# A trunk layer in split fp32: the order of down's steps, activations by two blocks, and two homes for the gates' x pairs

## The chip, the cores and the metric

The kernel runs on one core of one Trainium2 chip. The metric is device time in microseconds of one execution. The engines are named as the profile names them: PE (TensorE, matmuls; PEld its weight loads), DVE (VectorE), ACT (ScalarE), POOL (GpSimd) and SP (SyncE). On PE, DVE and ACT instructions run in program order; SP and POOL issue most of the DMA transfers, each from an in-order queue of its own, some are issued by ACT.

## What is computed

One layer of a transformer trunk for 512 tokens of width 2048, in float32:

```python
proj = rmsnorm(x, norm_mix) @ w_in        # q, k, v of two attentions, gates ga and gb (2048 columns each)
...
merged = sigmoid(ga) * (out_a @ w_branch_a) + sigmoid(gb) * (out_b @ w_branch_b)
x = x + merged @ w_out
u = rmsnorm(x, norm_ffn) @ w_up           # 2048 -> 2 x 5632
u = up[:, :-2] * cw[0] + up[:, 1:-1] * cw[1] + up[:, 2:] * cw[2] + conv_b
gate, val = split(u)
x = x + (silu(gate) * val) @ w_down       # 5632 -> 2048
```

Tokens lie along the free dimension (512), features along the 128 partitions.

## The kernel before

**Split operands.** Each float32 operand of a matmul is kept as two parts, hi (rounded to fp32r) and lo (the rest), and each product is three matmuls: hi by hi, hi by lo, lo by hi. Weights are split after loading by an ACT cast (`wh`) and a DVE subtraction (`wl`), L672 and L673, or L773 and L774 for plain tiles. Activations are split in the same way.

**Units.** From the gates on, the work of PE goes by units: 256 rows of a weight matrix by 512 columns, against a pair of feature tiles (256 features by 512 tokens). `tiles_by_halves` computes a unit plainly, in 2 x 4 x 2 blocks with three matmuls of 128x256 each, 48 in all. `products` does it by seven products of a Strassen-Winograd form, 7 x 2 x 3 = 42 matmuls of 128x256. For this the weights get three sums (`sums`, L630: two operations of 128x256 and one of 128x512 on DVE) and the activations come in seven forms, of which three are values and four sums (`forms`, L701 to L714). A run of units accumulates in one PSUM group per product; after its last unit `combine` (L810 to L850) makes the four quarters of the result out of the seven products, on ACT and DVE.

**Weights ahead of use.** `advance` moves the units through loading (`f`, SP queue, four buffers), sums and preparation (`prep`, two parities of w buffers, so that unit u + 2 is prepared when PE has finished unit u). A unit that is "kept" has its sums made early, in windows of the attention and branch stages: POOL fetches its weights (L645), DVE adds (L649), ACT stores the sums in DRAM (`sums...`). Later it loads 256 + 128 KB of weights and 512 KB of sums, in place of 512 KB of weights.

**Stages.** Attention and its projections (matmuls of 128x512), the gates' first three column blocks by plain 128x512 units, the other five blocks by `gate_products`, the branches and `w_out` by plain tiles, up (22 steps of 8 units, seven products), down (88 units).

- Gates: while the third block runs, `form_h` (L900) makes the seven forms of the eight x pairs: it scales a pair (ACT, L898), forms and splits it, and then lets POOL load the pair after the next into a buffer of the tag "a" (`load_x`, L890; two buffers). `gate_to_quad` (L884) multiplies PE's banks on DVE (L875), takes the sigmoid on ACT (L876) and stores.
- Up: each step writes eight blocks of activations (four values, four sums) of one pair to DRAM, `act0` to `act21`, by way of a convolution and a SiLU whose operations are queued behind the next step's units (L1054 to L1119).
- Down: the 22 pairs are in three parts (0 to 6, 7 to 13, 14 to 21), the output in four column blocks n. `load_act` brings a pair from DRAM into slots, one 128x256 block at a time (SP queue), and `split_act` (L1100 ACT, L1101 DVE) splits each block in place. Before, for each part the four blocks follow each other; three runs, (part 0, n 0), (part 0, n 3) and (part 1, n 3), are plain. The results of parts 0 and 1 are added to `total` in DRAM by accumulating POOL transfers (L1170); part 2 adds `total` on DVE and writes out.

**Order.** A scheduler with a timeline of its own orders the instructions; those under `keep` stay in the order in which the program issues them. The hooks `before(i)` and `after(i)` put loads and splits around unit i of a run.

Of the kernel before, what the change touches and what calls it, by code (L numbers as in the profile page):

```python
# [11 lines left out]
F32 = mybir.dt.float32  # L12
# [27 lines left out]
def trunk_kernel(  # L40
# [666 lines left out]
    def forms(src):  # L707
        y, one, two = form_sums(src)
        all_ = y[:, 0], y[:, 2], two[:, 1], one[:, 1], one[:, 0], two[:, 0], y[:, 3]
        res = [slot(F32R) for _ in all_]  # L710
        for i in (0, 1, 6, 4, 3, 5, 2):
            v, o = all_[i], res[i]
            nc.scalar.copy(o[:, :256], v)
            nc.vector.tensor_tensor(o[:, 256:], v, o[:, :256].bitcast(F32), ALU.subtract)  # L714
        return res

    def products(w, pairs, acts, evac, before=None, after=None, kept=(), total=None):

        n = len(pairs)

        def run():
            ps = []
            for i in range(n):
                if before:
                    before(i)
                u = next_unit()
                for f in (0, 1, 2, 3, 5, 6, 4) if i == n - 1 else range(7):
                    if i == 0:
                        ps.append(bank("mm"))
                    (wh, wl), a = u.parts[f], acts[i][f]  # L730
                    for m in range(2):
                        o, s = ps[f][:, m * 256:(m + 1) * 256], slice(m * P, (m + 1) * P)
                        mm(o, wh[:, s], a[:, :256], i == m == 0, False)
                        mm(o, wh[:, s], a[:, 256:], False, False)
                        last["pe"] = mm(o, wl[:, s], a[:, :256], False, i == n - 1 and m == 1)
# [45 lines left out]
    def tiles_by_halves(w, pairs, acts, evac, before=None, after=None):  # L781


        n = len(pairs)

        def run():
            ps = [bank("mm") for _ in range(4)]
            for i in range(n):
                if before:
                    before(i)  # L790
                u = next_unit()
                y = [acts[i][j] for j in (0, 7, 1, 6)]
                for m in range(4):
                    c = slice(m * P, (m + 1) * P)
                    for b in range(2):
                        first, last = i == b == 0, i == n - 1 and b == 1
                        wh, wl = u.hi[:, b, c], u.lo[:, b, c]
                        for t in range(2):
                            o, a = ps[m][:, t * 256:(t + 1) * 256], y[2 * b + t]
                            mm(o, wh, a[:, :256], first and t == 0, False)  # L800
                            mm(o, wh, a[:, 256:], False, False)
                            mm(o, wl, a[:, :256], False, last and t == 1)
                advance()
                run_queued(1)
                if after:
                    after(i)
            evac(ps)

        steps.append(run)
        for i in range(n):  # L810
            units.append(TilesByHalves(w[pairs[i]], len(units)))
            products_.append(units[-1])
# [75 lines left out]
            nc.gpsimd.dma_start(gate_a[m // 2], held["g"])  # L888

    def load_x(j):  # L890
        held[j] = quad("a")
        nc.gpsimd.dma_start(
            held[j], x_t[2 * j * P:(2 * j + 2) * P].rearrange("(a p) n -> p a n", p=P))

# [6 lines left out]
    def form_h():  # L901

        j = len(hf)
        if j < KD // 2:
            scale_x(j)
            hf.append(forms(held.pop(j)))
            if j + 2 < KD // 2:
                load_x(j + 2)

    def pre_forms():  # L910
        end_attention()
        load_x(0)
        load_x(1)

    def before_forms(kb):
        if 0 < kb < 7:
# [179 lines left out]
    def split_act(part, n):  # L1096
        if 0 <= n < len(parts[part]):
            for o in acts[part][n]:
                hi, lo = o[:, :256], o[:, 256:]
                keep(nc.scalar.copy(hi, lo.bitcast(F32)))  # L1100
                keep(nc.vector.tensor_tensor(  # L1101
                    lo, lo.bitcast(F32), hi.bitcast(F32), ALU.subtract))
# [42 lines left out]
    def down(part, n):  # L1145
        held = []

        def before(i):
            if n == 0 and part:
                load_act(part, 6 + i)  # L1150
            if part == n == 0 and i == 4:
                run_queued(1)
            if part == 0 and n == 1 and i == 1:
                queue.extend(unfinished)
            if part < 2 and n == 3:
                load_act(part + 1, i - 1)
            if part == 2 and i == 4:
                for j in range(2):
                    held.append(quad("ao"[j]))
                    dma(held[j], total[2 * n + j])  # L1160

        def after(i):
            if n == 0:
                split_act(part, i + (5 if part else 2))
            if part < 2 and n == 3:
                split_act(part + 1, i - 2)

        def evac(*results):
            for j, r in enumerate(results):
# [11 lines left out]
                keep(nc.scalar.copy(res[m // 2][:, m % 2], ps[m]))  # L1181
            evac(*res)

        if (part, n) in PLAIN:
            view = w_down.rearrange("(d b p) (s n) -> s d p b n", b=2, p=P, s=4)
            tiles_by_halves(view[n], parts[part], acts[part], evac_plain, before=before, after=after)
        else:
            view = w_down.rearrange("(d b p) (s h n) -> s d p b h n", b=2, p=P, s=4, h=2)
            products(view[n], parts[part], acts[part], evac if part < 2 else evac_total,
                     before=before, after=after, kept=(0, 1) if part and n == 0 else (),  # L1190
                     total=held if part == 2 else None)
# [73 lines left out]
```

## Time and profile before

| | |
|---|---|
| median of 3 runs | 2466.1 us (2464.73 to 2466.31) |
| the profiled execution | 2463.77 us, of which the span is 2462.0 |
| matmul, 128x256, seven products and plain | 277 ns each by its record (start to start is shorter, they overlap) |
| `f<-in_w_down`, 256 KB | 133 loads, median 4.0 us from issue to landing |
| `f<-sums`, 512 KB | 88 loads, median 5.8 us |
| `s<-act`, 128 KB | 168 loads, median 4.4 us |
| mean of all DMA | 214 GB/s |

Times in the profile are microseconds from the start of the span. A row of the groups gives line, engine, operation, out<-in, count, then busy time, mean ns of one, and the idle time of the engine just ahead of it with what ended it. A row of the timeline gives start, duration, engine, line, and in brackets how long the engine had been idle and which instruction released it. A row of the chain gives start and duration of a piece of the chain that ended last. The stages lie at 0 to 540 (attention), to 800 (gates), to 1203 (branches and `w_out`), to 2006 (up) and to the end (down).

### The profile page before, as it was taken

The page shows a single profiled execution, that of the slowest core. Times are in us where ns is not written, and L with a number is a line of the kernel's source. Part 1 is how long each engine was busy: PE and PEld are TensorE (multiplying, and loading weights), DVE is VectorE, ACT ScalarE, POOL GpSimd, SP SyncE. Part 2 cuts the span into 40 slices and gives each one's busy share as a digit, 9 for nine tenths or more (in the row PEclk, how much of TensorE's full clock was granted, in tenths as well). Part 3 has the DMA queues.
Part 4 walks back from the last instruction along what each step waited for, and adds up shares of the span by engine and source line. Part 5 has one row for each costly group of instructions (what it writes and reads, how often), then busy time and mean ns, then how long its engine had stood idle before and what let it go on. Part 6 is the DMA issues. An engine that isn't in the chain of part 4 may idle for free.

```text
span 2462.0 us, 45471 instructions
## 1 busy us (share of the span) xinstructions
PE 2436.6 (99%) x17430; PEld 2277.2 (92%) x17430; DVE 1860.1 (76%) x2939; ACT 1283.2 (52%) x1936; POOL 329.0 (13%) x406
## 2 busy tenths in 40 slices
PE   9999999999999999999999999999999999999998
PEld 7888888888899888888999999999999999999998
DVE  6788776635788656557878888888888878696897
ACT  5255554445545322334666566665665656463643
POOL 1414133000000111110011011110111101000000
PEclk9999999999999999999999999999999999999999
DMA  5767777435555677766588887887888897775853
GB/s 198 246 232 251 252 258 268 161 124 188 185 166 173 209 271 253 238 235 227 161 210 229 220 233 215 226 231 219 229 222 215 230 287 194 206 201 147 250 164 128
DMA packets 312362, 526.43 MB, mean 214 GB/s; under 512 B 27600, under 2 KB 179536, under 8 KB 312144
## 3 DMA queue, kind: packets, MB, share of 16 engines
q1 hardware_dynamic: 226320, 320.68, 41.3%
q0 software_dynamic: 48384, 128.91, 21.3%
q10 hardware_dynamic: 37440, 73.94, 7.9%
q8 instruction: 136, 2.23, 0.4%
q14 instruction: 82, 0.67, 0.1%
HBM read 378.80 MB, written 98.57 MB: 194 GB/s over the span
## 4 chain that ended last, share of the span: by engine, by line
PE 92%; DMA 3%; issue 3%; DVE 1%; ACT 1%; POOL 0%; SPq 0%; ACTq 0%; DVEq 0%; POOLq 0%
PE mm L76 88%; PE tr L76 2%; DMA f<-in_w_down 1%; PE tr L530 1%; DMA a<-in_x_t 1%; PE tr L369 0%; DMA s<-act 0%; DVE s L1101 0%; DMA sums<-s 0%; DMA f<-in_w_in 0%; ACT wh L672 0%; DMA s<-in_w_in 0%; DMA out_b<-o 0%; ACT hi L160 0%; PE tr L423 0%
## 5 line engine op out<-in xcount | busy, mean ns | idle before, releaser
L76 PE MATMUL mm<-s,wh 128*128 128x256 f32 (+1 forms) x9620 | 1719.6, 289 | 12.3 <-ACT wh L672 7.8
L76 PEld LDWEIGHTS mm<-s,wh 128*128 128x128 f32 x9620 | 1429.6, 188 | 55.8 <-ACT wh L672 9.2
L76 PE MATMUL mm<-s,wl 128*128 128x256 f32 (+1 forms) x4810 | 1227.1, 289 | 0.0
L76 PEld LDWEIGHTS mm<-s,wl 128*128 128x128 f32 x4810 | 841.4, 188 | 20.1
L672 ACT CAST wh<-f 128x1024 fp32r<-128x1024 f32 (+1 forms) x566 | 519.1, 943 | 484.7 <-PE mm L76 344.6
L673 DVE TENSOR_TENSOR wl<-f,wh 128x1024 fp32r<-128x1024 f32 (+1 forms) x566 | 610.6, 1088 | 188.7 <-ACT wh L672 185.9
L630 DVE TENSOR_TENSOR f<-f 128x256 f32<-128x256 f32 (+1 forms) x585 | 298.6, 510 | 4.7
L76 PE MATMUL mm<-hi,s 128*128 128x512 f32 x896 | 286.1, 394 | 5.6 <-ACT hi L160 5.6
L774 DVE TENSOR_TENSOR wl<-f,wh 128x1024 fp32r<-128x1024 f32 x85 | 104.1, 1225 | 172.5 <-ACT wh L773 167.4
L773 ACT CAST wh<-f 128x1024 fp32r<-128x1024 f32 x85 | 89.2, 1050 | 246.9 <-PE mm L76 213.9
L161 DVE TENSOR_TENSOR lo<-raw,hi 128x1024 fp32r<-128x1024 f32 (+1 forms) x97 | 117.7, 1214 | 122.8 <-ACT hi L160 116.9
L76 PEld LDWEIGHTS mm<-hi,s 128*128 128x128 f32 x896 | 168.1, 189 | 38.7 <-ACT hi L160 5.6
L76 PE MATMUL mm<-s,hi 128*128 128x512 f32 x640 | 195.8, 392 | 0.0
L160 ACT CAST hi<-raw 128x1024 fp32r<-128x1024 f32 (+1 forms) x97 | 101.2, 1043 | 157.6 <-PE mm L76 146.6
L76 PE MATMUL mm<-lo,s 128*128 128x512 f32 x448 | 175.6, 393 | 0.0
L76 PEld LDWEIGHTS mm<-s,hi 128*128 128x128 f32 x640 | 119.4, 188 | 24.1 <-ACT hi L160 0.3
L1070 POOL DMA_DIRECT2D o<-a x44 | 52.9, 1202 | 600.4 <-ACT a L1069 482.9
L76 PE MATMUL mm<-s,lo 128*128 128x512 f32 x320 | 120.8, 392 | 0.0
L649 DVE TENSOR_TENSOR s<-s 128x256 f32<-128x256 f32 x236 | 98.0, 421 | 5.8 <-DMA s<-in_w_in 3.4
L76 PEld LDWEIGHTS mm<-lo,s 128*128 128x128 f32 x448 | 84.6, 189 | 16.0
L1067 ACT ACTIVATE o<-u,smalls 128x512 f32<-128x512 f32 x88 | 71.5, 812 | 23.2 <-ACT wh L672 12.5
L645 POOL DMA_DIRECT2D s<-in_w_up x86 | 62.2, 725 | 95.0 <-DMA sums<-s 56.7
(148 smaller groups left out, 1860.0 us busy)
## 6 DMA issues: line engine op xcount, KB each, us to landing
f<-in_w_up SPq DMA_DIRECT2D x281, 256.0 KB, 3.8
f<-sums SPq DMA_DIRECT2D x88, 512.0 KB, 5.8
o<-a POOLq DMA_DIRECT2D x88, 511.0 KB, 7.1
f<-in_w_down SPq DMA_DIRECT2D x133, 256.0 KB, 4.0
raw<-in_w_in SPq DMA_DIRECT2D x63, 512.0 KB, 3.6
sums<-s ACTq DMA_DIRECT2D x118, 256.0 KB, 2.7
s<-in_w_up POOLq DMA_DIRECT2D x86, 256.0 KB, 5.3
s<-act SPq DMA_DIRECT2D x168, 128.0 KB, 4.4
```

What stands on the lines that cost most here:

```text
L76: return nc.tensor.matmul(o, l, r, start=start, stop=stop, skip_group_check=True).ins
L160: nc.scalar.copy(hi[:, c:c + n], self.raw[:, c:c + n])
L161: nc.vector.tensor_tensor(lo[:, c:c + n], self.raw[:, c:c + n], hi[:, c:c + n].bitcast(F32), ALU.subtract)
L630: add = lambda *args: keep(nc.vector.tensor_tensor(*args, ALU.add))
L645: keep(nc.gpsimd.dma_start(x, self.w[:, b]))
L649: add = lambda *args: keep(nc.vector.tensor_tensor(*args, ALU.add))
L672: keep(nc.scalar.copy(hi, f))
L673: keep(nc.vector.tensor_tensor(lo, f, hi.bitcast(F32), ALU.subtract))
L773: keep(nc.scalar.copy(hi, self.f))
L774: keep(nc.vector.tensor_tensor(lo, self.f, hi.bitcast(F32), ALU.subtract))
L1067: keep(nc.scalar.activation(self.o[:, m], u[:, m], AF.Identity, bias=cb[:, i:i + 1], scale=cw[:, i, 1:2]))
L1070: keep(nc.gpsimd.dma_start(self.o[:, :, 1:], first[:, :, :S - 1], accum_op=ALU.add))
```

## The change

It has five parts.

1. Down runs in ten steps, each with a column block n and one part or two: (0; 0), (1; 0), (2; 0), (3; 0, 1), (2; 1), (1; 1), (0; 1, 2), (1; 2), (2; 2), (3; 2). Where two parts stand, their 14 or 15 units accumulate in one PSUM group. Only (0; 0) is plain.
2. Activations of down are loaded by two blocks (128x512, 256 KB), three such and a single block for parts 1 and 2. A second slot takes the hi part of a wide block. For part 0 the values are loaded in up's last step and in the first run, the sums in the first and second. For the part that comes next, `LOADS` and `SPLITS` name the units of the merged run at which a pair is loaded and split.
3. Up's steps 1 to 20 keep units 2 and 3, not 2, 3 and 7. In down the kept units are 0, 1, 2 of (1; 0) and 5, 6, 7, 9, 10, 11, 12 of each merged run.
4. The x pairs of the gates are loaded into buffers of the tags "a" and "u" in turn, four ahead.
5. Slices of the split activations are handed on as (hi, lo) pairs; the work is the same.

```diff
-PLAIN = ((0, 0), (0, 3), (1, 3))
+LOADS = 1, 2, 3, 5, 6, 7, 8, 9
+SPLITS = 3, 4, 5, 7, 8, 9, 10, 11
+AHEAD_OF_SPLITS = 5, 6, 7, 9, 10, 11, 12
...
     def load_x(j):
-        held[j] = quad("a")
+        held[j] = quad("au"[j % 2])
...
-            if j + 2 < KD // 2:
-                load_x(j + 2)
+            if j + 4 < KD // 2:
+                load_x(j + 4)
...
-        load_x(0)
-        load_x(1)
+        for j in range(4):
+            load_x(j)
...
-    def load_act(part, n):
+    FORM_OF = 0, 7, 1, 6, 4, 3, 5, 2
+    VALUES, SUMS = (0, 2), (4, 6)
+
+    def load_act(part, n, blocks=None):
...
-            blocks = (0, 2, 7, 5, 4, 6, 3, 1)[:8 - (part == 2)]
-            tiles = [slot(F32R) for _ in blocks]
-            for o, i in zip(tiles, blocks):
-                dma(o[:, 256:].bitcast(F32), act[parts[part][n]][:, i])
-            acts[part].append(tiles)
+            if n == len(acts[part]):
+                acts[part].append(([None] * 8, deque()))
+            for b in blocks or (2, 4, 6, 0):
+                o = slot(F32R)
+                c = slice(0, 512) if b or not part else slice(256, 512)
+                dma(o[:, c].bitcast(F32), act[parts[part][n]][:, b:b + (c.stop - c.start) // 256])
+                acts[part][n][1].append((b, o, c))
...
-                load_act(0, i - 1)
+                load_act(0, i - 1, VALUES)
...
-                split_act(0, i - 6)
+                split_act(0, i - 6, 2)
...
-                 before=before, after=after, kept=(2, 3, 7) if s else range(8))
+                 before=before, after=after,
+                 kept={0: range(8), pairs_ff - 1: (2, 3, 7)}.get(s, (2, 3)))
...
         def before(i):
-            if n == 0 and part:
-                load_act(part, 6 + i)
+            if n == part == 0:
+                load_act(0, i, SUMS)
+            elif len(run) > 1 and i in LOADS:
+                load_act(run[1], LOADS.index(i))
...
         def after(i):
-            if n == 0:
-                split_act(part, i + (5 if part else 2))
-            if part < 2 and n == 3:
-                split_act(part + 1, i - 2)
+            if n == part == 0:
+                if i < 5:
+                    split_act(0, i + 2, 2)
+                split_act(0, i - 2, 2)
+            elif part == 0 and n == 1 and i in (1, 2):
+                split_act(0, i + 4, 2)
+            elif len(run) > 1 and i in SPLITS:
+                split_act(run[1], SPLITS.index(i))
...
-        if (part, n) in PLAIN:
+        if part == n == 0:
...
-    for part in range(3):
-        for n in range(4):
-            down(part, n)
+    for n, *run in ((0, 0), (1, 0), (2, 0), (3, 0, 1), (2, 1), (1, 1), (0, 1, 2), (1, 2), (2, 2), (3, 2)):
+        down(n, *run)
```

Three places in the instruction streams show how this moves work. Line numbers are two higher in the changed kernel up to here, and more further on; buffers are numbered anew.

The first is SP's queue at the end of up's last step. Before, with `f_22025` the weights of up's last unit, `s_...<-act2` the blocks of the pair 2, and `f_22109` the first weights of down:

```order
L73 DMA f_22025<-sums375_261 128x1024
L73 DMA s_22040<-act2_171 128x256
L73 DMA s_22041<-act2_171 128x256
L73 DMA s_22042<-act2_171 128x256
L73 DMA s_22043<-act2_171 128x256
L73 DMA s_22044<-act2_171 128x256
L73 DMA s_22045<-act2_171 128x256
L73 DMA s_22046<-act2_171 128x256
L73 DMA s_22047<-act2_171 128x256
L73 DMA f_22109<-in_w_down 128x2x512
```

The same place in the changed kernel, where `f_21998` is up's last unit and `f_22070`, `f_22134` down's first two:

```order
L75 DMA f_21998<-sums375_241 128x1024
L75 DMA s_22013<-act2_171 128x512
L75 DMA s_22015<-act2_171 128x512
L75 DMA f_22070<-in_w_down 128x2x512
L75 DMA s_22079<-act3_172 128x512
L75 DMA s_22081<-act3_172 128x512
L75 DMA f_22134<-in_w_down 128x2x512
```

Two loads of activations stand between two loads of weights, where eight stood.

The second is ACT at the border between the gates' plain units and the seven products. Before, with `o` the gate tiles, `a_6134` the x pair 7 and `wh_6168` the first weights of the seven products:

```order
L713 CAST s_6237<-a_6070 128x256
L876 ACTIVATE o_6204<-o_6204 128x512 x2
L898 ACTIVATE a_6134<-a_6134,gmix_86 128x512 x2
L672 CAST wh_6168<-f_5950 128x1024
L672 CAST wh_6172<-f_5950 128x768
```

And in the changed kernel, with `wh_6161` for the same weights:

```order
L715 CAST s_6230<-a_5939 128x256
L878 ACTIVATE o_6197<-o_6197 128x512 x2
L878 ACTIVATE o_6203<-o_6203 128x512
L674 CAST wh_6161<-f_5947 128x1024
L674 CAST wh_6165<-f_5947 128x768
```

The scaling of the last x pair no longer stands ahead of the weight casts; a third sigmoid does.

The third is DVE in the first run of down, between the weights of its second unit (`wl_22406` before) and those of its third. Before, the rows of up's last combine (L821, L843) are followed by eight splits (two are shown):

```order
L774 TENSOR_TENSOR wl_22406<-f_22185,wh_22405 128x1024
L821 TENSOR_TENSOR u_22401<-mm_21824,t_22403 128x2x256
L821 TENSOR_TENSOR t_22404<-t_22403,mm_21852 128x512
L821 TENSOR_TENSOR t_22403<-t_22404,u_22402 128x512
L821 TENSOR_TENSOR u_22401<-mm_21859,t_22403 128x2x256
L843 SCALAR_TENSOR_TENSOR t_22404<-mm_21845,t_22404 128x512
L821 TENSOR_TENSOR u_22402<-t_22404,u_22402 128x1024
L1101 TENSOR_TENSOR s_21956<-s_21956 128x256
L1101 TENSOR_TENSOR s_21957<-s_21957 128x256
```

And in the changed kernel, from the combine's last two operations to the weights of the third unit:

```order
L845 SCALAR_TENSOR_TENSOR t_22307<-mm_21842,t_22307 128x512
L823 TENSOR_TENSOR u_22305<-t_22307,u_22305 128x1024
L1113 TENSOR_TENSOR s_21941<-s_21941,s_22323 128x512
L1113 TENSOR_TENSOR s_21943<-s_21943,s_22326 128x512
L776 TENSOR_TENSOR wl_22386<-f_22190,wh_22385 128x1024
```

The combine keeps its place ahead of the splits; two wide splits stand where eight narrow ones stood.

More of the change, by code (lines that the diff above doesn't have):

```diff
@@ L729, in run @@
                         ps.append(bank("mm"))
-                    (wh, wl), a = u.parts[f], acts[i][f]
+                    (wh, wl), (ah, al) = u.parts[f], acts[i][f]
                     for m in range(2):
                         o, s = ps[f][:, m * 256:(m + 1) * 256], slice(m * P, (m + 1) * P)
-                        mm(o, wh[:, s], a[:, :256], i == m == 0, False)
-                        mm(o, wh[:, s], a[:, 256:], False, False)
-                        last["pe"] = mm(o, wl[:, s], a[:, :256], False, i == n - 1 and m == 1)
+                        mm(o, wh[:, s], ah, i == m == 0, False)
+                        mm(o, wh[:, s], al, False, False)
+                        last["pe"] = mm(o, wl[:, s], ah, False, i == n - 1 and m == 1)
                 advance(*(combine(ps, evac, total) if i == n - 1 else ()))
@@ L798, in run @@
                         for t in range(2):
[L799 to L802, printed above, removed]
+                            o, (ah, al) = ps[m][:, t * 256:(t + 1) * 256], y[2 * b + t]
+                            mm(o, wh, ah, first and t == 0, False)
+                            mm(o, wh, al, False, False)
+                            mm(o, wl, ah, False, last and t == 1)
                 advance()
@@ L1154, in before @@
                 queue.extend(unfinished)
-            if part < 2 and n == 3:
-                load_act(part + 1, i - 1)
-            if part == 2 and i == 4:
+            if run[-1] == 2 and i == len(pairs) - 4:
                 for j in range(2):
@@ L1182, in evac_plain @@
             evac(*res)
-        if (part, n) in PLAIN:
+        if part == n == 0:
             view = w_down.rearrange("(d b p) (s n) -> s d p b n", b=2, p=P, s=4)
-            tiles_by_halves(view[n], parts[part], acts[part], evac_plain, before=before, after=after)
+            tiles_by_halves(view[n], pairs, forms_at(), evac_plain, before=before, after=after)
         else:
             view = w_down.rearrange("(d b p) (s h n) -> s d p b h n", b=2, p=P, s=4, h=2)
-            products(view[n], parts[part], acts[part], evac if part < 2 else evac_total,
-                     before=before, after=after, kept=(0, 1) if part and n == 0 else (),
-                     total=held if part == 2 else None)
+            kept = AHEAD_OF_SPLITS if len(run) > 1 else (0, 1, 2) if (n, part) == (1, 0) else ()
+            products(view[n], pairs, forms_at(), evac if run[-1] < 2 else evac_total,
+                     before=before, after=after, kept=kept,
+                     total=held if run[-1] == 2 else None)
     for s in range(pairs_ff):
         up(s)
-    for part in range(3):
-        for n in range(4):
-            down(part, n)
+    for n, *run in ((0, 0), (1, 0), (2, 0), (3, 0, 1), (2, 1), (1, 1), (0, 1, 2), (1, 2), (2, 2), (3, 2)):
+        down(n, *run)
     for st in steps:
```

32 lines of the change are left out of this document (22 added, 10 removed).

## The prediction

> **What bounds the kernel now.** I read the page first, then the chain of waits in order of time, then PE's waits, then windows around the places that these name.
>
> ```profile
> span 2462.0 us, 45471 instructions
> PE 2436.6 (99%) x17430; PEld 2277.2 (92%) x17430; DVE 1860.1 (76%) x2939; ACT 1283.2 (52%) x1936; POOL 329.0 (13%) x406
> PE 92%; DMA 3%; issue 3%; DVE 1%; ACT 1%; POOL 0%; SPq 0%; ACTq 0%; DVEq 0%; POOLq 0%
> ...
> 623.31 560.11 PE mm L76 x3384
> ...
> 1266.71 739.20 PE mm L76 x6504
> 2006.32 6.04 DMA f<-in_w_down
> ```
>
> PE is the bound: busy 99% and 92% of the chain, and the whole up stage is one unbroken piece of 6504 matmuls in 739.20 us. That gives the price of a 128x256 matmul in steady work: 739.20/6504 = 0.1137 us. So two things can make the kernel shorter: fewer matmuls, and the places where PE does not run at that rate. The next rows find these places (stretch, length, busy us of PE, PEld, DVE, ACT and POOL with counts, granted clock, share of the DMA engines, GB/s).
>
> ```profile
> 700.00:800.00 100.00, 100.00 (x883) 100.00 (x882) 83.32 (x113) 50.49 (x60) 3.20 (x6) 1.00 0.52 169
> 2000.00:2100.00 100.00, 95.57 (x790) 93.83 (x789) 79.42 (x139) 59.97 (x110) 10.71 (x10) 0.95 0.81 219
> 2100.00:2200.00 100.00, 99.37 (x868) 98.66 (x867) 75.30 (x133) 53.95 (x99) 3.44 (x4) 1.00 0.72 212
> 2300.00:2400.00 100.00, 99.10 (x870) 98.71 (x869) 95.05 (x160) 51.90 (x78) 6.09 (x10) 1.00 0.63 189
> ```
>
> A full 100 us holds 883 matmuls. The start of down (2000 to 2100) has 790: 93 x 0.1137 = 10.6 us lost. 2100 to 2200 loses 15 (1.7 us), 2300 to 2400 loses 13 (1.5 us). Fourth place, the border between the gates' plain units and their seven products:
>
> ```profile
> 616.69 0.72 POOL L892 DMA_DIRECT2D a<-in_x_t  x1 [5.46 <-ACT s L713]
> 620.99 1.33 ACT L898 ACTIVATE a<-a,gmix 128x512 f32<-128x512 f32 x2 [1.08 <-DMA a<-in_x_t]
> 622.23 1.77 ACT L672 CAST wh<-f 128x1024 fp32r<-128x1024 f32 x2
> 623.31 1.01 PE L76 MATMUL mm<-s,wh 128*128 128x256 f32 x3 [6.14 <-ACT wh L672]
> 620.00:623.30 3.30, 0.00 (x0) 0.00 (x0) 0.45 (x2) 2.31 (x4) 0.56 (x1) 0.50 0.45 185
> 623.30:626.70 3.40, 3.39 (x16) 3.39 (x17) 2.77 (x3) 3.40 (x5) 0.56 (x1) 0.50 0.11 10
> 626.80:630.20 3.40, 3.40 (x31) 3.40 (x31) 3.35 (x8) 1.24 (x4) 0.00 (x0) 1.00 0.96 326
> ```
>
> PE waits 6.14 us for a weight cast, which stands in ACT's order behind the scaling of x pair 7, which waits for a load that POOL issued only at 616.69, when the forms of the pair before had freed a buffer. Then 3.4 us run at half clock: 16 matmuls where the next stretch has 31, 15 x 0.1137 = 1.7 us more. Together 7.8 us. The other losses lie in the attention stage, whose instructions the change leaves in their order.
>
> **Fewer matmuls.** Two of three plain runs of seven units become seven products: 14 units x (48 - 42) = 84 matmuls, 84 x 0.1137 = **-9.5 us**. These lie on PE, so all of it counts. Nine combines stay nine; two plain evacuations and four accumulations of 512 KB go, which lay beside PE.
>
> **Gates.** Two homes for x put four loads ahead in place of two. ACT's order then has x pair 7's scaling well before the last plain unit ends; between that end and the weight cast stand three sigmoids.
>
> ```profile
> 618.02 0.63 ACT L876 ACTIVATE o<-o 128x512 f32<-128x512 f32 x1 [0.51 <-DVE o L875]
> ```
>
> The cast itself waits for nothing of PE, but the sigmoids do: each follows a product on DVE that reads one of PE's last banks. Three of the four stand ahead of the cast, so I expect it to end about 1.2 us after PE does (the third sigmoid is then under way, 0.63, and the cast's own 1.05 lies partly behind PE's last matmuls), with full clock. Ends: 0 left (all early), or 1.2 + 1.7 left if the clock still drops. I take 1.2: **-6.6 us**.
>
> **Start of down.** Where its 10.6 us come from:
>
> ```profile
> 1989.52 8.03 SPq L73 DMA_DIRECT2D s<-act  x8
> 1997.64 1.53 SPq L73 DMA_DIRECT2D f<-in_w_down  x1
> 2005.72 1.05 ACT L773 CAST wh<-f 128x1024 fp32r<-128x1024 f32 x1 [5.82 <-DMA f<-in_w_down]
> 2007.91 2.54 ACT L1100 CAST s<-s 128x256 fp32r<-128x256 f32 x8
> 2008.35 0.84 PE L76 MATMUL mm<-s,wh 128*128 128x256 f32 x2 [1.77 <-ACT s L1100]
> 2005.80:2009.10 3.30, 1.45 (x10) 1.06 (x9) 1.99 (x4) 3.30 (x7) 0.80 (x1) 1.00 1.10 266
> 2009.20:2012.50 3.30, 2.03 (x8) 1.63 (x8) 1.91 (x6) 1.28 (x6) 0.30 (x1) 0.50 1.11 347
> 2012.60:2015.90 3.30, 2.49 (x11) 2.19 (x11) 2.35 (x3) 3.30 (x8) 0.00 (x0) 0.50 1.10 279
> 2016.00:2019.40 3.40, 3.40 (x18) 3.40 (x18) 3.19 (x5) 1.41 (x5) 0.00 (x0) 0.50 1.02 366
> ```
>
> Down's first weights are requested at 1997.64, behind eight act loads that held SP's queue for 8.03 us, with the DMA engines full. They land at 2005.6, and PE, done with up by then, finds the first splits not made; the second weights are as late; three stretches run at half clock. The change puts two act loads where eight stood (blocks 0 and 2 in one DMA each), so the first weights can be requested about 8.03 x 6/8 = 6 us earlier and are there before PE ends. Splitting two 128x512 takes ACT and DVE less than eight 128x256, by rows of the same operation elsewhere:
>
> ```profile
> L939 ACT CAST s<-s 128x512 fp32r<-128x512 f32 x16 | 9.7, 622 | 10.6 <-DMA s<-out_b 7.3 <-DMA s<-out_a 3.2
> L940 DVE TENSOR_TENSOR s<-s 128x512 fp32r<-128x512 f32 x16 | 10.7, 687 | 5.6 <-ACT s L939 5.6
> L1101 DVE TENSOR_TENSOR s<-s 128x256 fp32r<-128x256 f32 x168 | 58.2, 422 | 2.6 <-ACT s L1100 2.6
> L774 DVE TENSOR_TENSOR wl<-f,wh 128x1024 fp32r<-128x1024 f32 x21 | 25.7, 1225 | 47.8 <-ACT wh L773 44.5 <-DMA s<-act 3.3
> L821 DVE TENSOR_TENSOR u<-mm,t 128x512 f32<-128x512 f32 x24 | 16.5, 688 | 4.9 <-PE mm L76 4.4
> L821 DVE TENSOR_TENSOR u<-t,u 128x1024 f32<-128x1024 f32 x8 | 9.8, 1222 | 0.3
> ```
>
> What is late next is DVE. Counted from PE's end E, the second unit's wl (after an ACT cast of 1.05) ends near E + 2.4; then DVE's order has up's last combine, five operations of 0.69 and one of 1.22, 4.7 us; then the first split of the second unit, 0.69: E + 7.8. PE reaches that product after 48 + 4 matmuls, at E + 5.9. I expect a wait of some 1.7 us. At the border from the plain run to the next, two more ACT splits stand before the plain copies (0.62 each by the row of L939); I let PE see 0.7 us of these 1.24. Ends for both: 0 and 2.4 + 1.7. I take 2.4: **-8.2 us**.
>
> The rule on the clock bears on this remnant. The Trainium skill, "TensorE: Matmul & The Clock Gate", Part 1, has the clock halve after an idle window of about 3.4 us and come back after a busy one; by it a wait of 1.7 us keeps the clock full and the sum stands. The trace speaks against it in part: the clock was 0.50 from 2009.2 although the stretch before had PE busy 1.45 of 3.30 us. By the trace a remnant may cost another 1.7 us.
>
> **Starts of parts 1 and 2.** The 1.7 and 1.5 us were lost where eight 128x256 splits per pair, the sums of weights and a combine came together on DVE and ACT. Inside a merged run there is no combine, each pair takes four splits, and seven of its units have their sums made early. I leave 1.2 of 3.2: **-2.0 us**. Ends: all gone, or nothing gone and 3 more for each run (below).
>
> **What is costed at nothing.** Twenty units of up sum in place: two of 0.42 and one of 0.69, 1.5 us each, 31 us of DVE.
>
> ```profile
> 1266.70:2005.90 739.20, 739.19 (x6506) 739.19 (x6507) 623.05 (x826) 475.49 (x620) 94.17 (x79) 1.00 0.85 227
> L630 DVE TENSOR_TENSOR f<-f 128x256 f32<-128x256 f32 x158 | 66.8, 423 | 2.0
> L630 DVE TENSOR_TENSOR f<-f 128x512 f32<-128x512 f32 x79 | 54.2, 687 | 0.0
> L673 DVE TENSOR_TENSOR wl<-f,wh 128x1024 fp32r<-128x1024 f32 x89 | 108.8, 1223 | 41.8 <-ACT wh L672 40.2 <-PE mm L76 1.4
> L673 DVE TENSOR_TENSOR wl<-f,wh 128x768 fp32r<-128x768 f32 x89 | 84.9, 954 | 3.6 <-ACT wh L672 3.6
> ```
>
> DVE is busy 623 of 739 us in up, so 116 are free, 5.3 in each of 22 steps; 1.5 fit. If none hid, it would be +31. Each of these units loads 512 KB in place of 896 (256 and 128 of weights, 512 of sums), so DMA gets lighter there. In a merged run a unit lasts PE 42 x 0.1137 = 4.77 us. With a split (three of 0.69, one of 0.42: 2.5) and wl (1.22 + 0.95) DVE needs 4.7 where the sums are early, 6.2 where not. One to three units in a run are of the second kind, up to 1.4 us over each. DVE stood idle 41.8 us ahead of the first wl in 89 units, so it is ahead as a rule: 0 to 3 us for a run, and I take 0.
>
> **Sum:** -9.5 - 6.6 - 8.2 - 2.0 = -26.3 us. The profiled execution took 2463.8 (its span and 1.8 outside); the median of the runs is 2466.1, 2.3 above. 2466.1 - 26.3 = 2439.8, so **2440 us**.
>
> **Rivals.**
> (a) The clock still drops at one or both borders: +1.7 or +3.4, 2442 to 2444. For it: the row at 2009.2. Against: PE was busy less than half of the stretch before that, and each remnant is one gap of 1 to 2 us with full work on both sides.
> (b) About half of the losses stay, since what is late next (DVE's combine, the sigmoids) is later than I count: half of 16.8 back, 2448.
> (c) The change does only what its matmuls say; each wait moves to another releaser: 2466.1 - 9.5 = 2456.6. Against it: both long waits have one cause each (queue order), and that is taken away.
> (d) Slower: the merged runs become bound by DMA. Seven units in each ask for 896 KB of weights with their early sums and for 896 KB of activations (three loads of 256 KB and one of 128), together 1.84 MB in 4.77 us. The nearest stretch with both kinds of load moved:
>
> ```profile
> 2130.00:2180.00 50.00, 49.98 (x438) 49.59 (x436) 37.52 (x79) 32.59 (x74) 1.88 (x3) 1.00 0.95 269
> ```
>
> At 269 GB/s such a unit takes 6.8 us, 2.05 too many. Three in a row, a light one (0.52 MB, 2.8 us to spare), then four: 3 x 2.05 - 2.8 + 4 x 2.05 = 11.6 us behind. Loads are asked for about four units ahead (19 us), of which preparation uses one or two, so 9.5 to 14 us of cover: it decides from there. If the cover were gone for all 14 units, 29 us come back (2469); with PE waiting 2 us in each unit the clock, by the row of 2009.2, could stay at half, 14 x 4.77 = 67 more, 2536. Against it: 366 GB/s at 2016 and 326 at 626.8, by which the backlog is a few us.
>
> **How the numbers follow.** The forecast with its own spread (2434 to 2443) has 0.60, (a) 0.14, (b) 0.12, (c) 0.05, (d) 0.05, of which 0.03 beyond 2471, and 0.04 for waits that I have not seen, either way. The range 2433 to 2452 holds the forecast, (a), (b) and the lower ends of the unknown costs. Differences under 0.2% (4.9 us) can't be told from no change. Faster 0.92, same 0.05, slower 0.03.
>
> **What would show it.** Right: 84 matmuls fewer; PE's wait at the first seven products near 1 us with the clock at 1.0 after it; down's first weights landed before up ends and a wait for a DVE split of 1 to 2 us; no row below 880 matmuls in 100 us inside the merged runs; up still at 113.7 ns a matmul. Wrong: a wait for f or act loads or for sums in the merged runs, a clock of 0.50 there, or up no longer one piece.

## The result and the profile after

The changed kernel takes **2443.07 us** (median of 4 runs, 2441.52 to 2443.53) against 2465.94 before (2464.73 to 2466.31): ratio 0.9907, 95% interval 0.989 to 0.9924. That is 22.9 us less, inside the range, and 3.1 us above the 2440 that were predicted. The two profiled executions lie 20.8 us apart in span. The page of the changed kernel, and from the chain of its waits the last long piece:

```profile
span 2441.2 us, 45026 instructions
PE 2422.1 (99%) x17346; PEld 2264.5 (93%) x17346; DVE 1881.9 (77%) x2911; ACT 1280.2 (52%) x1862; POOL 314.1 (13%) x394
...
2014.22 417.19 PE mm L78 x3662
```

PE has 84 matmuls fewer, and from 2014 to the end of down it is one piece of 3662 matmuls; before it was four pieces with waits between them. The same stretches as before (columns as in the prediction):

```profile
600.00:700.00 100.00, 96.18 (x757) 92.91 (x756) 75.69 (x121) 54.84 (x85) 5.45 (x9) 0.98 0.54 181
2000.00:2100.00 100.00, 97.35 (x845) 96.40 (x845) 80.19 (x112) 60.00 (x86) 9.97 (x10) 1.00 0.87 242
2100.00:2200.00 100.00, 100.00 (x882) 100.00 (x881) 85.42 (x124) 55.39 (x76) 3.44 (x4) 1.00 0.71 224
2300.00:2400.00 100.00, 100.00 (x883) 100.00 (x882) 91.33 (x139) 46.16 (x57) 4.37 (x8) 1.00 0.53 171
```

Against the counts of before: 845 for 790 at the start of down (55 x 0.1137 = 6.3 us), 882 for 868 and 883 for 870 behind it (3.1 us). For the gates' border the row of before is

```profile
600.00:700.00 100.00, 93.86 (x737) 90.58 (x736) 75.55 (x121) 55.94 (x88) 5.41 (x9) 0.97 0.55 180
```

so 20 matmuls or 2.3 us. With the 9.5 of the matmuls themselves (84 x 0.1137) that is 21.2, less 0.7 that up now loses (below): 20.5 of the 20.8 us are found.

PE's waits after the change, all of 0.3 us and more:

```profile
PE mm L78 <- ACT hi L162: 5.3, 1, 5.3
PE mm L78 <- ACT wh L674: 3.8, 1, 3.8
PE mm L78 <- DVE s L1113: 1.5, 2, 1.2
PE mm L78 <- ACT s L1112: 1.2, 1, 1.2
```

The first is the wait ahead of the kernel's first matmuls, which the change leaves alone. The second is the gates' border, where 1.2 were predicted. The timeline of the changed kernel there:

```profile
616.99 0.69 DVE L877 TENSOR_TENSOR o<-mm,row 128x512 f32<-128x512 f32 x1
617.92 1.88 DVE L877 TENSOR_TENSOR o<-mm,row 128x512 f32<-128x512 f32 x3
618.64 1.23 ACT L878 ACTIVATE o<-o 128x512 f32<-128x512 f32 x2 [0.30 <-DVE o L877]
619.78 1.77 ACT L674 CAST wh<-f 128x1024 fp32r<-128x1024 f32 x2
620.86 1.39 PE L78 MATMUL mm<-s,wh 128*128 128x256 f32 x6 [3.82 <-ACT wh L674]
621.20:624.50 3.30, 3.30 (x18) 3.30 (x17) 3.19 (x4) 2.55 (x4) 0.54 (x1) 0.50 0.55 190
```

No x pair stands in the way any more. But the three sigmoids ahead of the cast wait for DVE's multiplications of PE's last banks, one after the other, and the cast of the weights starts only at 619.78, 2.7 us after PE's end. The clock halves once more.

The other two waits are the start of down:

```profile
1987.07 0.38 SPq L75 DMA_DIRECT2D f<-in_w_down  x1
2004.35 1.34 ACT L1078 ACTIVATE a<-u,smalls 128x512 f32<-128x512 f32 x2 [4.40 <-DMA o<-a]
2005.59 1.12 ACT L1112 CAST s<-s 128x512 fp32r<-128x512 f32 x2
2006.24 0.38 PE L78 MATMUL mm<-s,wh 128*128 128x256 f32 x1 [1.15 <-ACT s L1112]
2013.48 1.29 DVE L1113 TENSOR_TENSOR s<-s 128x512 fp32r<-128x512 f32 x2
2014.22 0.39 PE L78 MATMUL mm<-s,wh 128*128 128x256 f32 x1 [1.16 <-DVE s L1113]
```

Down's first weights are asked for at 1987.07, 10.6 us sooner than before. The 1.16 at 2014.22 is the wait behind up's last combine that was predicted at 1.7. The 1.15 at 2006.24 was not foreseen: the first splits stand on ACT behind a step of the convolution (L1078) that waits for a POOL transfer.

### The profile page after: what moved, and what is told of

It is laid out like the page before. It is cut to its first block, busy times and chain, and to the rows that moved or that the text cites. A ratio compares the mean times of both kernels' runs of the same rounds, so it can differ in the third digit from the quotient of the medians.

```text
span 2441.2 us, 45026 instructions
## 1 busy us (share of the span) xinstructions
PE 2422.1 (99%) x17346; PEld 2264.5 (93%) x17346; DVE 1881.9 (77%) x2911; ACT 1280.2 (52%) x1862; POOL 314.1 (13%) x394
## 5 line engine op out<-in xcount | busy, mean ns | idle before, releaser
L78 PE MATMUL mm<-s,wh 128*128 128x256 f32 (+1 forms) x9564 | 1689.4, 289 | 6.7 <-ACT wh L674 3.8
L78 PEld LDWEIGHTS mm<-s,wh 128*128 128x128 f32 x9564 | 1400.3, 188 | 48.7 <-ACT wh L674 5.1
L78 PE MATMUL mm<-s,wl 128*128 128x256 f32 (+1 forms) x4782 | 1184.1, 288 | 0.0
L78 PEld LDWEIGHTS mm<-s,wl 128*128 128x128 f32 x4782 | 817.6, 188 | 20.0
L674 ACT CAST wh<-f 128x1024 fp32r<-128x1024 f32 x594 | 547.7, 941 | 517.3 <-PE mm L78 400.1
L675 DVE TENSOR_TENSOR wl<-f,wh 128x1024 fp32r<-128x1024 f32 x594 | 642.8, 1087 | 171.1 <-ACT wh L674 161.6
L632 DVE TENSOR_TENSOR f<-f 128x256 f32<-128x256 f32 (+1 forms) x639 | 325.4, 509 | 7.6 <-DMA f<-in_w_down 2.3
L776 DVE TENSOR_TENSOR wl<-f,wh 128x1024 fp32r<-128x1024 f32 x71 | 87.0, 1225 | 134.8 <-ACT wh L775 131.6
L775 ACT CAST wh<-f 128x1024 fp32r<-128x1024 f32 x71 | 74.4, 1048 | 199.0 <-PE mm L78 185.4
L1072 POOL DMA_DIRECT2D o<-a x44 | 52.9, 1202 | 584.5 <-ACT a L1071 517.6
L1080 POOL DMA_DIRECT2D o<-a x44 | 52.8, 1201 | 175.5 <-ACT a L1078 161.6
```

What stands on the lines that cost most here:

```text
L78: return nc.tensor.matmul(o, l, r, start=start, stop=stop, skip_group_check=True).ins
L632: add = lambda *args: keep(nc.vector.tensor_tensor(*args, ALU.add))
L674: keep(nc.scalar.copy(hi, f))
L675: keep(nc.vector.tensor_tensor(lo, f, hi.bitcast(F32), ALU.subtract))
L775: keep(nc.scalar.copy(hi, self.f))
L776: keep(nc.vector.tensor_tensor(lo, self.f, hi.bitcast(F32), ALU.subtract))
```

## The experiments

Each is an edit of the changed kernel; e1 to e4, e5 to e8 and e9 to e12 ran together; the kernel before, run beside each group, took 2464.3, 2464.33 and 2464.08 us, so the groups can be compared. Times are medians, with the lowest and highest run. "Lost" below is PE's time over the rate of 0.1137 us a matmul, by the start times of the trace.

**e1, the changed kernel again.**

> The changed kernel as it is, as the measure for the other three. 2441.5 to 2443.5 us, as in its first runs. In its trace the border of the gates again loses 5.9 us (4.0 idle, the rest at half clock) and the start of down 4.0 us.

2441.93 us (2441.05 to 2442.01; ratio to before 0.9906, 0.9891 to 0.9922). Lost at the border of the gates 5.0, at the start of down 3.2 us: each somewhat less than in the first profile (5.9 and 4.0). In all the traces whose edit leaves the gates alone that border loses 4.8 to 7.1 us, so what one profile says of one place is good to about 1 us.

**e2, one home for x.**

```diff
-        held[j] = quad("au"[j % 2])
+        held[j] = quad("a")
...
-            if j + 4 < KD // 2:
-                load_x(j + 4)
+            if j + 2 < KD // 2:
+                load_x(j + 2)
...
-        for j in range(4):
+        for j in range(2):
             load_x(j)
```

> Only the x pairs are put back: one home, two loads ahead. Theory (the second home took away the wait for x, and the wait for the sigmoids then came last): PE's wait at the first seven products is 6.1 us again in place of 3.8, the loss there 8.0 in place of 5.9, the time 2.2 us longer than e1. Rival (the second home did nothing, the wait at that place differs between programs anyway): within 0.5 us of e1.

2445.51 us (2444.54 to 2446.28), 3.6 more than e1. Its timeline at the border:

```profile
620.22 1.33 ACT L900 ACTIVATE a<-a,gmix 128x512 f32<-128x512 f32 x2 [0.84 <-DMA a<-in_x_t]
622.54 3.35 PE L78 MATMUL mm<-s,wh 128*128 128x256 f32 x14 [5.16 <-ACT wh L674]
```

The wait for x is back, 5.2 us, and two stretches at half clock (14 matmuls in 3.35 us). Lost there: 7.8, which is 2.8 more than e1. So the second home did what it was for, and its worth is 2 to 4 us, since the sigmoids came last next.

**e3 and e4, what stands ahead of the first weights.** The diff is that of e4: the sigmoids are queued, and `keep` holds the DVE multiplications behind the weights in program order; e3 has it without that `keep`. (Lines shift: L877 is L888 there.)

```diff
-        gate(m, ps, held["g"][:, m % 2])
-        if m % 2:
-            nc.gpsimd.dma_start(gate_a[m // 2], held["g"])
+        keep(nc.vector.tensor_tensor(held["g"][:, m % 2], ps, rows["m"], ALU.mult))
+        if m % 2:
+            def finish(g=held["g"]):
+                keep(nc.scalar.activation(g, g, AF.Sigmoid))
+                nc.gpsimd.dma_start(gate_a[m // 2], g)
+
+            queue.append(finish)
```

> The four sigmoids of the last plain block are queued behind the first weight casts of the seven products; the DVE multiplications stay where they are. Theory (two engines hold PE one after the other: ACT's sigmoids hold wh, and behind them DVE's four multiplications hold wl): PE goes on 1.1 us after the last plain matmul, makes the matmuls that need only wh, and then waits for wl until about 4 us after that end; the gain over e1 is 0.3 to 1.5 us, or up to 2.5 if the clock stays full. Rival 1 (only the sigmoids hold PE): the wait falls from 3.8 to about 1.1 us in all and 4.4 us are gained. Rival 2 (the weight buffers come free only at PE's end and later): nothing is gained.

2438.79 us (2437.79 to 2440.2), 3.1 less than e1. PE's two waits there in e3:

```profile
617.56 1.92 PE L78 MATMUL mm<-s,wh 128*128 128x256 f32 x14 [0.21 <-ACT wh L674]
620.69 0.39 PE L78 MATMUL mm<-s,wl 128*128 128x256 f32 x1 [1.21 <-DVE wl L675]
```

Two engines in turn, as the theory had it, but cheaper: PE had 14 matmuls to do with wh alone, and the clock stayed full. The gain is above the 2.5 that were given as the upper end.

> As e3, and the DVE multiplications too stand behind the first wl. Theory: one wait of 1.0 to 1.3 us at the border, clock 1.0 after it, 4 to 4.6 us less than e1 (2438.6). Rival (the clock drops all the same after such a gap): 2.5 to 3 us less. Rival (the banks that the multiplications free late hold the fifth product): a second wait of 1 to 2 us, gain 2 to 3.

2437.29 us (2436.85 to 2438.55), 4.6 less than e1: the gain that was expected, without the one wait of 1.0 to 1.3 us that was expected beside it. In e4 the order at the border is wh, wl, then the multiplications, and the stretch has no gap left:

```profile
616.13 3.46 ACT L674 CAST wh<-f 128x1024 fp32r<-128x1024 f32 x4
617.20 2.10 DVE L675 TENSOR_TENSOR wl<-f,wh 128x1024 fp32r<-128x1024 f32 x2 [0.44 <-ACT wh L674]
619.21 2.48 DVE L888 TENSOR_TENSOR o<-mm,row 128x512 f32<-128x512 f32 x4
600.00:700.00 100.00, 99.98 (x801) 96.57 (x800) 80.17 (x128) 56.00 (x85) 5.46 (x9) 1.00 0.54 181
```

**e5, splits one unit sooner,** and **e6, e4 and e5 together.**

```diff
-                split_act(0, i - 6, 2)
+                split_act(0, i - 5, 2)
...
-                if i < 5:
-                    split_act(0, i + 2, 2)
+                if i < 4:
+                    split_act(0, i + 3, 2)
```

> Each pair of part 0 is split one unit earlier, so that the second pair's splits stand ahead of up's last combine on DVE and the first pair's ahead of the last convolution steps on ACT. Theory (at the start of down PE waits twice, 0.5 to 1.3 and 0.6 us for the first splits, which stand on ACT behind a step of the convolution that waits for a POOL transfer, and 1.3 us for the second pair's split, which stands on DVE behind the combine): both waits go, the loss there falls from 3.2 (e1) to 0.3 to 0.8 us, time 2439.2. Rival (the combine, now later, holds PSUM banks or the next weights, and the wait only moves): loss 2 us or more, less than 1 us gained.

2441.02 us (2440.15 to 2441.11), 0.9 less than e1: between theory and rival. The three waits are gone, and one came:

```profile
2006.63 0.98 PE L78 MATMUL mm<-s,wh 128*128 128x256 f32 x4 [0.46 <-ACT wh L775]
```

The second unit's weights now stand on ACT behind the same convolution step. Lost at the start of down: 1.6 in place of 3.2.

> e4 and e5 together. The two places lie 1400 us apart, so the gains add up: 4.6 + 2.7 less than e1 (2441.9), 2434.6 us. Rival (the earlier end of the gates moves a later stage into a worse place): 2436 to 2437.5.

**2435.91 us** (2434.76 to 2436.44; ratio to before 0.9884, 0.987 to 0.9897), 6.0 less than e1 and the fastest of all; 1.4 less than e4 alone. That is 1.3 more than the sum that was expected, which took e5 to be worth 2.7; with the 0.9 that e5 gained the sum is 5.5.

**e7 and e9, the same bytes in narrow loads.** The diff is that of e9, where the second of each two goes by POOL's queue; in e7 both go by `dma`, SP's.

```diff
-                dma(o[:, c].bitcast(F32), act[parts[part][n]][:, b:b + (c.stop - c.start) // 256])
+                for k in range((c.stop - c.start) // 256):
+                    d = slice(c.start + k * 256, c.start + k * 256 + 256)
+                    issue = dma if k == 0 else nc.gpsimd.dma_start
+                    issue(o[:, d].bitcast(F32), act[parts[part][n]][:, b + k])
```

> Every two-block load is issued as two loads of 128x256 again; splits, order and bytes stay. Theory (what keeps down's first weights back is the bytes ahead of them on SP's queue, not the number of loads): the loss at the start of down stays within 1 us of e1's 3.2, the time within 1.5 us of 2441.9; the first weights of down are asked for at most 3 us later. Rival (each load costs SP about 1 us): four loads ahead of each weight cost 2 us more each, the first weights come 4 to 8 us later and PE waits 3 us or more; in the merged runs weights come late too.

2454.63 us (2452.24 to 2457.24), **12.7 more** than e1. (The profiled execution is the slowest of the five, 15.4 above e1's.) The start of down is nearer to the theory than to the rival: 4.8 lost between 2000 and 2050, 1.6 more than e1 where the theory allowed 1, and the first weights are asked for at 1988.45, 1.4 us later. The loss lies in the merged runs, where the rival had it too: 13.7 us from 2150 to 2350. PE's first wait, by its releaser, and DVE's behind it, in e7:

```profile
PE mm L78 <- DVE wl L675: 8.7, 8, 2.6
...
2176.38 0.69 DVE L632 TENSOR_TENSOR f<-f 128x512 f32<-128x512 f32 x1 [3.83 <-DMA f<-in_w_down]
```

DVE waits for weights that have not landed. The same 40 us of the first merged run in the changed kernel, in e7 and in e9 (the last two columns are the share of the DMA engines and GB/s):

```profile
2120.00:2160.00 40.00, 40.00 (x354) 40.00 (x354) 34.55 (x49) 25.18 (x37) 1.22 (x2) 1.00 1.01 338
...
2120.00:2160.00 40.00, 39.28 (x345) 39.08 (x345) 32.96 (x47) 23.54 (x34) 1.72 (x2) 1.00 0.93 278
...
2120.00:2160.00 40.00, 37.85 (x326) 37.06 (x325) 30.75 (x44) 24.13 (x35) 11.56 (x21) 1.00 1.00 327
```

And the SP queue's DMA (packets, MB moved, share of the engines' time) there, in the changed kernel, e1, e7 and e9:

```profile
q1 hardware_dynamic: 6743, 12.39, 86.0%
...
q1 hardware_dynamic: 6648, 12.10, 86.8%
...
q1 hardware_dynamic: 7681, 10.00, 77.5%
...
q1 hardware_dynamic: 6364, 9.27, 67.4%
```

Two things go with 278 in place of 338. The engines are 0.93 full in place of 1.01, while SP issues ten loads a unit and not seven. And a MB of SP's takes the engines longer: 77.5/10.00 in e7 is 12% above 86.0/12.39, though only 8% above e1, which is the same program as the changed kernel. That narrow pieces as such are slower to move is not shown: SP's loads in e9, narrow too, take within 2% of e1's share for each MB, and by the trace's packet records a piece of 1 KB took 48 ns in e7 in these 40 us, about half of the 93 ns of a 2 KB piece in the changed kernel. What took longer in e7 was the weights' 2 KB pieces, 120 ns.

> As e7 (two narrow loads for each wide one), but the second of each two is issued by POOL, so SP issues as many activation loads as in e1. e7 lost 13.7 us in the two merged runs (2150 to 2350), where e1 lost nothing. Theory (the DMA engines move narrow pieces more slowly: 304 against 379 GB/s from 2150 to 2160): the bytes and pieces are those of e7, so 8 to 14 us stay lost in the merged runs, time 2450 to 2456. Rival (SP's time to issue is what runs out): under 2 us lost there, time 2441.5 to 2444.

2448.87 us (2447.73 to 2451.1), 6.9 more than e1, 5.8 less than e7; lost in the merged runs about 7. Neither theory alone: with the issuing shared the engines are full again (1.00) and about half of the loss goes. In the 40 us above they move 327 GB/s, nearly as much as with wide loads, and PE waits all the same, so the size of the pieces doesn't explain the other half. POOL's queue with its own timing came in with the edit; the cause of this half stays open.

The Trainium skill, "DMA: Bandwidth & Descriptors", section "Issuing engines are not separate DMA queues", has it that issuing on several engines saves only the sequencer's time to start them, which is usually small beside the transfer itself. Here handing a part of the loads to POOL gave back 5.8 us, in a queue that feeds PE.

**e8, all blocks of part 0 in up's last step.**

```diff
-                load_act(0, i - 1, VALUES)
+                load_act(0, i - 1)
...
-                split_act(0, i - 6, 2)
+                split_act(0, i - 6)
```

and in down's first run all four splits of a pair two units ahead, no loads of sums.

> In up's last step all four wide loads of a pair are issued again, with all its splits two units before use, as before the change, in wide pieces. Theory (bytes): 1 MB a unit and the weights beside it saturate the DMA engines again; down's first weights land near PE's end of up, splits of all forms stand ahead of the second unit's, and the loss at the start of down is 7 to 10 us, 4 to 6 more than e1. Rival (it was the number of loads): the loss is within 1 us of e1's.

2449.5 us (2448.35 to 2450.54), 7.6 more than e1; lost around the start of down (1985 to 2055) 11.9 us, 8.5 more than e1: more than the theory had, and not within reach of the rival. Wide loads alone don't save this time; bringing and splitting the values first does. But it isn't down's first weights that come late. SP and PE in e8:

```profile
1988.63 0.38 SPq L75 DMA_DIRECT2D f<-in_w_down  x1
...
1991.08 1.88 PE L78 MATMUL mm<-s,wh 128*128 128x256 f32 x14 [1.73 <-ACT wh L674]
2008.67 0.48 PE L78 MATMUL mm<-s,wh 128*128 128x256 f32 x1 [2.08 <-ACT s L1112]
```

These weights are asked for at 1988.63, nearly as early as in the changed kernel (1987.07) and 9 us earlier than in the kernel before (1997.64). In e7 and in e8 four loads stand where eight stood, in e8 with all their bytes, and both bring the request forward; so it isn't the bytes ahead of it that hold it back. PE waits in e8 for a weight cast in up's last units, and at the start of down for the first splits, which are now four in a row behind the convolution step; then the clock is at half for 6.8 us. The edit moves loads and splits together, so their shares are not separated.

**e10, three kept units in up** (the first edit), and **e11, none in the merged runs** (the second).

```diff
-                 kept={0: range(8), pairs_ff - 1: (2, 3, 7)}.get(s, (2, 3)))
+                 kept=range(8) if s == 0 else (2, 3, 7))
...
-AHEAD_OF_SPLITS = 5, 6, 7, 9, 10, 11, 12
+AHEAD_OF_SPLITS = ()
```

> Up's steps keep three units again (2, 3, 7), so 20 more sums are made early and 1.5 us of DVE leave each step. Theory (DVE has the room, so these sums cost nothing where they are): within 0.6 us of e1's 2441.9, up's rate stays 113.7 ns a matmul. Rival (the change paid for them): 1 us or more faster than e1; rival (the early fetches and the 384 KB more of each load are the dearer way): 1 us or more slower.

2444.05 us (2443.27 to 2444.69), 2.1 more than e1, but not for up's sake. Loads of early sums in down, in the changed kernel and in e10:

```profile
f<-sums SPq DMA_DIRECT2D x17, 512.0 KB, 6.3
...
f<-sums SPq DMA_DIRECT2D x1, 512.0 KB, 6.3
```

The loads of early sums in all are 84 in the changed kernel and 88 in e10, as before the change: there seems to be room for some 88 units, filled in the program's order, and 20 more of up's crowd out 16 of down's. So e10 too has merged runs without early sums, and it loses 2.3 us there. Up itself is the better for it: one piece, 113.66 ns a matmul in e10 (the first row, from its chain) against 113.77 in the changed kernel (the second, 741.90/6521).

```profile
1263.85 709.15 PE mm L78 x6239
...
1263.00:2004.90 741.90, 741.66 (x6521) 741.00 (x6520) 648.53 (x885) 476.46 (x623) 94.87 (x79) 1.00 0.82 218
```

Over 6521 matmuls that is about 0.7 us, the price of the sums that were costed at nothing.

> No unit of the merged runs has its sums early; each loads 512 KB and is summed on DVE. Theory (DVE is the bound of a unit with splits and sums: 6.2 us against PE's 4.77): seven units in each run fall behind by 1.4 us, less the lead of about one unit: 4 to 6 us lost in each merged run, 2450 to 2454, waits for DVE's wl or sums. Rival (DMA is what is short there, and 384 KB less a unit help): no loss, 2442 or less.

2446.83 us (2445.33 to 2448.17), 4.9 more than e1. Lost in the merged runs: 3.3 us, not 8 to 12; 2 us more of the profiled time are at the border of the gates, which the edit doesn't touch (there two stretches ran at half clock, not one). So the early sums of the merged runs are worth 2 to 3 us by e10 and e11. The expectation summed DVE's durations, which overstate what a unit costs it, if not by all of the difference: its operations overlap at their ends (in e10 one of 0.69 starts at 2316.23 and the next at 2316.83).

**e12, one more plain run.**

```diff
-        if part == n == 0:
+        if part == 0 and n in (0, 2):
```

> The run of column block 2, part 0 is plain again: 7 units of 48 matmuls in place of 42. Theory (PE's matmuls count in full): 42 x 0.1137 = 4.8 us more than e1, 2446.7. Rival (plain units, which need no sums and no combine, give part of it back): 1 to 3 us more.

2446.76 us (2444.72 to 2448.5), 4.8 more than e1: what 42 matmuls take, counted in full. (Its runs spread over 3.8 us.)

## Why the prediction came out as it did

| step of the prediction | predicted | in the profiles | by experiment |
|---|---|---|---|
| 84 fewer matmuls | -9.5 | -9.5 | e12: 4.8 for 42 |
| gates | -6.6 | -2.3 | e2: 3.6 lost when undone, 2.8 of it at the border |
| start of down | -8.2 | -6.3 | e8: 7.6 lost when all blocks are loaded and split at once again |
| starts of parts 1 and 2 | -2.0 | -3.1 | e7, e10, e11: lost again with narrow loads or late sums |
| sums in up | 0 | +0.7 | e10 |
| sum | -26.3 | -20.5 | |

- **Matmuls.** Right: the page counts 84 fewer, and e12 gives their price.
- **Gates: the step that was most off.** The mechanism was right (x's load away, sigmoids last), the size of the remnant wrong: "I expect it to end about 1.2 us after PE does (the third sigmoid is then under way". It is not under way then: it waits for DVE's third multiplication, and these come one after the other from PE's end on. The wait was 3.8 us in place of 1.2 and brought a stretch at half clock, which the prediction had only as an upper end and as rival (a); with both, more was left than that upper end of 2.9. e3 and e4 show the chain by taking it away.
- **Start of down.** The queue kept the first weights back, as said: they are asked for 10.6 us sooner, and PE no longer waits for them. But the early request is not enough: in e8 it is early too, and 8.5 us more are lost. The rest comes of taking a pair's values first, in loads and splits. The wait behind the combine came as predicted (1.16 for 1.7), and the 0.7 at the plain run's end did not. Missed was the split behind ACT's convolution step; e5 shows that step, by what it then held in the split's place.
- **Merged runs.** Nothing is lost there, where 1.2 us were left over. No run puts the old order of parts and column blocks back, so that the merging does this is read from the traces and not tested by itself. Rival (d) did not come with the change as it is, but with narrow loads (e7) the merged runs do wait for weights, 13.7 us in the profile. The prediction costed the wide loads at the start of down, where narrow ones cost 1.6 us in e7, and not in the merged runs. Its 269 GB/s were no limit of the engines: wide loads moved 338.
- **Up.** Costed at nothing; 0.7 us.
- **The median.** The profiled execution of before lay 2.2 us below its median, that of the changed kernel at its median (2441.2 and 1.8 outside the span against 2443.07). So the medians differ by 2.1 us more than the profiles, which hid part of the error above (in e1's group they differ by 22.4). The terms of the sum are 5.8 us short together, the time only 3.1: that the number came so near is in part luck. 2443.07 lies at the end of the forecast's own spread (2434 to 2443) and within rival (a)'s (2442 to 2444); the clock did drop at one border, as (a) has it, but the longer wait ahead of it weighs more.

## What to carry to other kernels

When a wait at a border goes, follow the whole chain of what stands ahead of the next instruction on its engine, down to what each of these waits for: an instruction that stands early in the order is not early if it reads the last result of the stage before. Queue the work that nothing waits for (here sigmoids and the multiplications that feed them) behind the first weights of the next stage: 4.6 us for ten lines. Where a run takes weights and activations at once, look at the number of loads and at who issues them, not only at bytes: the same bytes in half as wide pieces cost 12.7 us.

## What the runs showed of the hardware

The clock halved without an idle stretch of 3.4 us. By the clock's records each stay at half clock amid the work lasts 3.41 us or a multiple of it (6.83 and 10.24 in the kernel before), and from one drop to the next it is whole multiples too (619.95 to 2009.18 there, 407 times 3.413): within a trace the clock changes on a fixed grid. The first two groups of rows are the stretches of this grid around a drop in e7 and e8, the third the one ahead of a drop in the kernel before. The last three have gaps too, in e8, the changed kernel and e3, and the clock stayed full after them:

```profile
2174.60:2177.90 3.30, 0.80 (x8) 0.60 (x6) 1.52 (x3) 0.67 (x1) 0.00 (x0) 1.00 0.68 248
2178.00:2181.40 3.40, 3.40 (x16) 3.40 (x17) 3.40 (x7) 0.81 (x2) 0.00 (x0) 0.50 0.50 158
...
2005.40:2008.70 3.30, 1.22 (x12) 1.02 (x10) 1.61 (x3) 3.30 (x7) 1.20 (x1) 1.00 1.09 319
2008.80:2012.10 3.30, 2.81 (x12) 2.52 (x13) 3.21 (x5) 3.30 (x7) 0.00 (x0) 0.50 1.09 293
2012.20:2015.60 3.40, 3.40 (x18) 3.40 (x18) 3.26 (x5) 0.89 (x2) 0.00 (x0) 0.50 1.09 267
2015.60:2019.00 3.40, 3.40 (x31) 3.40 (x31) 2.28 (x4) 1.03 (x2) 0.00 (x0) 1.00 1.05 402
...
2005.80:2009.20 3.40, 1.55 (x10) 1.07 (x9) 2.09 (x4) 3.40 (x8) 0.90 (x1) 1.00 1.10 270
...
1988.30:1991.70 3.40, 1.67 (x15) 1.47 (x14) 0.64 (x1) 3.40 (x5) 1.20 (x1) 1.00 1.01 372
...
2003.60:2007.00 3.40, 1.91 (x16) 1.51 (x14) 0.78 (x2) 2.65 (x5) 1.02 (x1) 1.00 1.07 304
...
618.10:621.50 3.40, 2.19 (x18) 1.99 (x17) 3.40 (x6) 1.83 (x3) 0.00 (x0) 1.00 0.00 0
```

PE was busy 0.80 and 1.22 us of 3.3 and 1.55 of 3.4 before a drop, and 1.67 to 2.19 of 3.4 where none came. In these programs, then, the clock falls after a stretch with PE busy less than something between 46% and 49%. It comes back after a stretch with PE busy throughout; in e8 2.81 us of 3.3 were not enough. The Trainium skill, "TensorE: Matmul & The Clock Gate", Part 1, speaks of an idle window of about 3.4 us; by that none of these drops should have come, since PE's longest wait was 2.6 us in e7 and 2.1 in e8. The grid does not start with the program, so the same wait may cost one stretch or two: the 3.8 us at the border of the gates end ahead of a new stretch in the changed kernel (at 620.86, the stretch begins at 621.2) and cost one; in e11 they reach into the stretch from 619.8 on, and two run at half clock.
